# Where the shift row of the first attention values is kept, how it is added, and when the decay table is loaded, in a hybrid decoder block

## The chip, the cores and the metric

The kernel runs on one core of a Trainium2 chip, as one program with one launch. The metric is the device time of that core in microseconds; the runs of the kernel before gave 2195.38, 2193.04 and 2194.74 us, with a median of 2194.74 us. All data is float32; a matmul operand is split into a high and a low part, and every product is made as three matmuls.

## The reference

One decoder block on a sequence of 1024 tokens with a model width of 1024. A conditioning vector gives a shift and a scale for each channel. Two mixers read the same modulated input: chunkwise retention (4 heads) and dilated window attention (3 groups of 4 heads). Their outputs are gated, merged and projected, and an MLP with squared ReLU follows.

```python
def modulate(h, shift, scale):
    return h * (1 + scale[:, None, :]) + shift[:, None, :]

mod = jax.nn.silu(c) @ w_ada[l] + b_ada[l]
sh1, sc1, g1, sh2, sc2, g2 = jnp.split(mod, 6, axis=-1)
h = modulate(rms_norm(x, norm1_g[l]), sh1, sc1)
x = x + g1[:, None, :] * token_mixer(h, w_in[l], ...)
...
proj = h @ w_in
...
inner_decay = jnp.where(rel >= 0, jnp.exp(log_g[:, None, None] * jnp.maximum(rel, 0.0)), 0.0)
s = jnp.einsum('bhid,bhjd->bhij', qi, ki) * inner_decay[None]
```

Two places matter here. The attention values of the first group are `h @ w`, and since the shift is the same for every token, `shift @ w` is one row of 512 numbers that is added to all 1024 rows of the values. And retention multiplies its scores by a table of decays, one 128 x 128 block for each of the four heads.

## The kernel before

**Order.** The order of every engine is written out by hand; nothing is scheduled by a program. Each engine takes its instructions in that order and waits where an operand or a buffer is not ready. The DMAs of the weights, stores and copies are issued from SP's queue, one after another; DMAs that add to their destination (accumulating ones) are issued from GpSimd's queue. An issue that waits holds all issues behind it.

**Buffers.** Up to the retention, the tiles of 128 x 1024 come from `x4` (line 344): a ring of 26 buffers in SBUF that all kinds of tiles share. A new tile takes a buffer that was let go, and its first writer waits for the last readers of the tile that had it, DMAs among them. Which tile gets which buffer follows from the order in which tiles are made and let go. `decay` (128 x 512) is a tile of its own in another pool and keeps its place.

**First values** (`first_values` and `more_values`, to about 180 us). The values of attention group 0 are computed from the input before the shift is known to it, and stored to `va_d[0]` in DRAM, eight blocks of 128 rows x 512. Meanwhile `shift_rows` (line 996) sums on VectorE, over the eight blocks of input channels, weight row times shift into `decay`, which serves as scratch for that; so `decay` holds 128 partial rows. `more_values` then makes further values in eleven products of four parts. In the last product, after its first part, `shift_out` runs: one matmul with ones adds up the 128 partial rows and gives the shift row in all 128 partitions of a PSUM tile, two ScalarE copies put it twice, side by side, into the tile `shw` from the ring, and four accumulating DMAs of GpSimd add it to `va_d[0]`, 256 rows each.

**Pairs** (`queries_keys`, from about 180 us). 18 pairs of projections follow, numbered `q` from 0: queries and keys of the retention, queries of the attention, gates. A pair is made in a block scheme with seven products, in the order `11, s1, s3, s2, 12, 22, s4`, of 12 matmuls each, into the PSUM tiles `qap`. `Blocks.run` (line 302) does, for each product: its matmuls, then the preparation of weights some products ahead (sums of weight blocks on VectorE into `qas`, line 249; the high part by a ScalarE cast, line 254; the low part on VectorE, line 264, into `qaw`), then `post` (line 281). `post` copies and adds up PSUM tiles (`qat`, lines 286, 292 and 293) and hands finished blocks to `a_out` (line 1167), which writes the tiles `qa` (ScalarE, line 1182; VectorE, line 1184) and stores them. `a_load` (line 1142) loads the weight tiles `wa` two pairs ahead, and `copy_block` (line 531) sends copies and sums of other weights (`wrvs`, `wros`) to DRAM on the side, of which `quarter_sums` (line 539) are accumulating DMAs on GpSimd. In `after` (line 1226), at product 22 of pair 0, the decay table is loaded into `decay`, where the retention reads it (line 654).

Of the kernel before, what the change touches and what calls it, by code (L numbers as in the profile page):

```python
# [14 lines left out]
ALU = mybir.AluOpType  # L15
AX = mybir.AxisListType

P = 128
# [4 lines left out]
C = 128  # L23
NC = S // C
DV = 512
# [115 lines left out]
def block_kernel(ctx, tc, io, stop=None, dbg=None):  # L141
    nc = tc.nc
# [26 lines left out]
    def ps_s(name, shape=(P, 512)):  # L169
        return PS["p"].tile(list(shape), F32, tag="s", bufs=PS["n"], name=name)  # L170
# [168 lines left out]
    decay = right0.tile([P, H * C], F32, name="decay")  # L339
# [4 lines left out]
    def x4(name, dt=F32):  # L344
        return xpool.tile([P, 1024], dt, tag="x", bufs=26, name=name)
# [143 lines left out]
    def drain(gen):  # L489
        for _ in gen:  # L490
            pass
# [39 lines left out]
    def copy_block():  # L531

        if copies:
            d, src, n, j = copies.pop(0)
            nc.sync.dma_start(d[n][j], io[src][WB[n], j])
            if n == "s3":
                quarter_sums(d, io[src], j)
# [14 lines left out]
    def gn_signs():  # L552
        for i, v in enumerate((VC_GNG, VC_GNB)):
            nc.vector.tensor_copy(gnv[i][:, :16], vec[:, v:v + 16])
            nc.vector.tensor_scalar_mul(gnv[i][:, 16:], vec[:, v:v + 16], -1.0)
# [214 lines left out]
    va_d = [dram.tile([S, 512], F32, name=f"vad{g}") for g in range(3)]  # L770
# [233 lines left out]
    def shift_out():  # L1004

        ps = ps_s("shw")
        nc.tensor.matmul(ps, ones.to_broadcast([P, P]), decay, start=True, stop=True)
        t = x4("shw")
        for j in range(2):
            nc.scalar.copy(t[:, 512 * j:512 * j + 512], ps)  # L1010
        for i in range(4):
            dst = va_d[0][2 * C * i:2 * C * (i + 1)].rearrange("(a p) x -> p a x", p=P)
            nc.gpsimd.dma_start(dst, t.rearrange("p (a x) -> p a x", a=2), accum_op=ALU.add)

    def more_values(ahead):

# [24 lines left out]
        def pair_load(q):  # L1041
# [18 lines left out]
            (9, 0): [(sums_of_h, "t4", [0, 1]), (nc.sync.dma_start, cs, io["cossin"])],  # L1060
            (9, 1): [(sums_of_h, "t4", [2, 3])], (9, 2): [(late_low,), (pair_load, 0)],
            (10, 0): [(pair_load, 1), (shift_out,)],
        }
        for i in range(len(USEQ)):
# [77 lines left out]
    def a_load(q, part):  # L1142
        pair = PAIRS[q]
        src = io[{"g": "w_gate2", "a": "w_aq"}.get(pair[0]) or f"w_r{pair[1]}"]
        i = 2 * pair[1] + pair[2] if pair[0] == "a" else pair[-1]
        if q == 0 or q % 2 == 0 and part == 2:
            r = x4(f"wa{q}{part}")
        else:
            r = wraw.tile([P, 1024], F32, tag="raw", name=f"wa{q}{part}")
        nc.sync.dma_start(r, src[2 * i + part - 1])  # L1150
        BA.raw[q, part] = r
# [44 lines left out]
    def rotate(q):  # L1196

        _, t, h = PAIRS[q]
        u, v = BA.t[q]
        for hf in range(2):  # L1200
            hs = slice(512 * hf, 512 * hf + 512)
            x1, x2, cos, sin = OA[q][0][:, hs], OA[q][1][:, hs], cs[:, 0, hs], cs[:, 1, hs]
            for f, o, x, y in ((nc.vector.tensor_mul, u, x2, sin), (nc.vector.tensor_mul, v, x1, sin),
                               (nc.vector.tensor_mul, x1, x1, cos), (nc.vector.tensor_mul, x2, x2, cos),
                               (nc.vector.tensor_sub, x1, x1, u), (nc.vector.tensor_add, x2, x2, v)):
                f(o, x, y)
                yield
        for i in range(2):
            nc.sync.dma_start(qk_d[h][:, 2 * (t == "k") + i], OA[q][i])
# [4 lines left out]
    def queries_keys(ahead):  # L1214
        for _ in range(4):
            copy_block()
        sums = [(q, n) for q in range(NA) for n in ORDER][4:]

        def before(q, n):
            if n == ORDER[0] and q + 2 < NA:  # L1220
                for part in (1, 2):
                    a_load(q + 2, part)

        turns = []

        def after(q, n):

            if q == 0 and n == "22":
                gn_signs()
            if q == 0 and n == "22":  # L1230
                nc.sync.dma_start(decay, io["decay"])
            if n in ("s1", "s2", "12"):
                copy_block()
            if turns:
                next(turns[0], None) or None
            if n == ORDER[-1] and PAIRS[q][0] == "r":
                while turns:
                    drain(turns.pop())
                turns.append(rotate(q))
            if q == NA - 1 and n in ("s1", "s4"):  # L1240
                v_load(n == "s4")
            if q == NA - 1 and n == "12":
                v_base_load(0)
            if q == NA - 1 and n in ("12", "22"):
                v_w(0, int(n == "22"))
                v_low(0, int(n == "22"))

        BA.run([(q, n) for q in range(NA) for n in ORDER], sums, before, after, lambda q, n: n == "s2", lambda q: 1 if q == 0 else 2)
        while turns:
            drain(turns.pop())  # L1250
        values(ahead)
# [13 lines left out]
    def v_load(i):  # L1265

        hp, n = VSEQ[i]
        for j in range(2):
            lo = V["w", i, j] = v_place(i, "l", j)
            nc.sync.dma_start(fv(lo), wv_d[n][2 * hp + j])  # L1270

    def v_w(i, j):
        lo, hi, sign = V["w", i, j], v_place(i, "h", j), float(VPLAN[VSEQ[i][1]][1])
        nc.scalar.activation(hi, fv(lo), AF.Copy, scale=sign)
        V["w", i, j] = hi, lo
        V["low", i, j] = lo, hi, sign

    def v_low(i, j):
        lo, hi, sign = V.pop(("low", i, j))
        if sign > 0:  # L1280
            nc.vector.tensor_sub(lo, fv(lo), fv(hi))
        else:
            nc.vector.scalar_tensor_tensor(lo, fv(lo), -1.0, fv(hi), op0=ALU.mult, op1=ALU.subtract)
# [47 lines left out]
    def v_base_load(hp):  # L1331

        for j in range(2):
            V["m", hp, j] = t = x4(f"vm{hp}{j}")
            nc.sync.dma_start(t.rearrange("p (a b) -> p a b", a=2), m11_d[hp][:, 2 * j:2 * j + 2])

    def values(ahead):
        last = len(VSEQ) - 1
        for i, (hp, n) in enumerate(VSEQ):
            if i + 2 <= last:  # L1340
                v_load(i + 2)
            for p in range(4):
                v_mm(i, p)
                if V["post"]:
                    v_post(*V["post"].pop())
                V["post"].append((i, p))
                if i == 3 and p == 0:
                    v_base_load(1)
                if n == "s1" and p > 0:
                    v_base(hp, p - 1)  # L1350
                if n == "s2" and p == 0:
                    v_base(hp, 3)
                if p < 2 and i < last:
                    v_w(i + 1, p)
                    if p:
                        v_low(i + 1, 0)
                if p == 2 and i < last:
                    v_low(i + 1, 1)

                if i == last - 2 and p == 2:  # L1360
                    fetch(0)
                if i == last - 2 and p == 3:
                    first["release"]()
                if i == last - 1 and p in (1, 2):
                    jit_qk(p - 1)
                if i == last - 1 and p == 3:
                    ahead(2)
                if i == last and p == 0:
                    for m in range(4):
                        nc.gpsimd.dma_start(hh[2 * m][:, 512:], h12_d[m][:, 0])  # L1370
                        nc.gpsimd.dma_start(hl[2 * m][:, 512:], h12_d[m][:, 1])
        v_post(*V["post"].pop())
        open_ret()
        chunk_tiles()
        for g in (1, 2):
            fetch(g)
        R["sl"] = R["p"].tile([P, 2, DV], F32R, name="statel")
        R["sh"] = R["p"].tile([P, 2, DV], F32R, name="stateh")
        R["state"] = R["p"].tile([P, 2, DV], F32, name="state")
        banks(False)  # L1380
# [1423 lines left out]
```

## Time and profile before

| | value |
|---|---|
| runs, us | 2193.04, 2194.74, 2195.38 (median 2194.74) |
| the profiled execution's own time, us | 2194.82 |
| its span, first to last instruction, us | 2193.0 |
| mean granted TensorE clock | 0.996 |
| DMA packets, bytes | 160897, 416.78 MB |
| TensorE's first projections / retention / last stage | from 180 us / about 644 us / to the end of the span |

The profile is of one execution. In the views, a row of the timeline has the start, the duration, the engine and line, the operation with the tile it writes and the one it reads, and in brackets how long the engine had been idle before and what ended that. PE is TensorE's matmuls, PEld its weight loads, DVE is VectorE, ACT is ScalarE, POOL is GpSimd; SPq and POOLq are the queues that issue DMAs. Matmuls are pipelined: a row's duration overlaps the next, and the distance between two starts is what a matmul costs. The granted clock is a share of full speed.

### The profile page before, as it was taken

How to read it: one execution, taken by the hardware profiler on the slowest of the kernel's cores; microseconds unless marked ns; L12 is line 12 of the kernel's file. 1: busy time of each engine (PE TensorE's matmuls, PEld its weight loads, DVE VectorE, ACT ScalarE, POOL GpSimd, SP SyncE). 2: the span in 40 equal slices, each digit the busy share in tenths (PEclk: the TensorE clock that was granted, in tenths of full speed). 3: DMA queues.
4: the chain of work that ended last, by engine and by line, in shares of the span. 5: the costliest groups of instructions: out<-in, count | busy, mean ns of one | idle time of the engine just before them, and what ended most of it. 6: DMA issues, size and time to landing. Idle time of an engine off the chain costs nothing. (4 is left out here: it accounts for less than half of the span.)

```text
span 2193.0 us, 27323 instructions
## 1 busy us (share of the span) xinstructions
PE 2160.1 (98%) x10084; PEld 1794.8 (82%) x10084; DVE 1492.3 (68%) x2333; ACT 942.8 (43%) x1730; POOL 165.0 (8%) x196
## 2 busy tenths in 40 slices
PE   8998999999999999999999999999999999999998
PEld 6887788888878888888888888888778888888887
DVE  6984777775457878865565654777876665877855
ACT  5542322323434544544644634534454445533413
POOL 0001111100012221111100000001000000000003
PEclk9999999999999999999999999999999999999999
DMA  9869899834675555557763274654154435745322
GB/s 384 285 210 269 273 312 266 248 117 181 231 280 174 177 192 199 181 182 182 175 188 102 83 259 166 241 180 152 59 182 148 146 147 183 256 138 174 114 87 77
DMA packets 160897, 416.78 MB, mean 190 GB/s; under 512 B 27765, under 2 KB 55676, under 8 KB 157692
## 3 DMA queue, kind: packets, MB, share of 16 engines
q1 hardware_dynamic: 151416, 368.67, 47.5%
q0 software_dynamic: 9024, 46.14, 9.7%
q8 instruction: 79, 1.29, 0.2%
q14 instruction: 54, 0.44, 0.1%
q10 hardware_dynamic: 324, 0.23, 0.0%
HBM read 319.93 MB, written 156.13 MB: 217 GB/s over the span
## 5 line engine op out<-in xcount | busy, mean ns | idle before, releaser
L207 PE MATMUL qap<-hh,qaw 128*128 128x512 f32 x216 | 84.6, 392 | 2.4 <-DVE qat L293 2.4
L211 PE MATMUL qap<-hh,qaw 128*128 128x512 f32 x216 | 84.7, 392 | 0.0
L209 PE MATMUL qap<-hl,qaw 128*128 128x512 f32 x216 | 84.6, 392 | 0.0
L617 POOL TENSOR_TENSOR j<-qk,j 128x512 fp32r<-128x512 f32 x32 | 43.3, 1352 | 428.3 <-ACT j L616 410.3
L2124 POOL TENSOR_TENSOR accnf<-accnf,sqnf 128x256 f32<-128x256 f32 (+1 forms) x18 | 16.6, 921 | 609.6 <-ACT sqnf L2120 609.6
L2228 ACT ACTIVATE a<-a 128x512 f32<-128x512 f32 x48 | 30.3, 631 | 73.7 <-DVE a L2227 73.7
L1544 ACT ACTIVATE P<-P,ng 128x128 f32<-128x128 f32 (+1 forms) x96 | 41.9, 438 | 36.9 <-DVE ng L1541 33.3
L2436 ACT CAST w2h<-w2s 128x512 fp32r<-128x512 f32 x36 | 22.4, 622 | 79.4 <-DVE w2s L2474 79.4
L264 DVE TENSOR_TENSOR fw<-w1r,fw 128x512 fp32r<-128x512 f32 x48 | 32.9, 688 | 33.5 <-ACT fw L254 33.5
L207 PEld LDWEIGHTS qap<-hh,qaw 128*128 128x128 f32 x216 | 40.8, 189 | 11.3 <-DVE qat L293 2.8
L207 PE MATMUL fp<-h2h,fw 128*128 128x512 f32 x128 | 50.0, 391 | 0.0
L1959 DVE TENSOR_TENSOR rwl<-rwl,rwh 128x1024 fp32r<-128x1024 f32 x25 | 30.2, 1220 | 29.0 <-ACT rwh L1989 29.0
L211 PE MATMUL fp<-h2h,fw 128*128 128x512 f32 x128 | 49.8, 389 | 0.0
L209 PE MATMUL fp<-h2l,fw 128*128 128x512 f32 x128 | 49.8, 389 | 0.0
L207 PE MATMUL roa<-rh,rwl 128*128 128x512 f32 x128 | 49.8, 389 | 0.0
L209 PE MATMUL roa<-rl,rwh 128*128 128x512 f32 x128 | 49.8, 389 | 0.0
L211 PE MATMUL roa<-rh,rwh 128*128 128x512 f32 x128 | 49.8, 389 | 0.0
L652 ACT COPY sm<-sT 128x128 f32<-128x128 f32 x32 | 8.5, 265 | 93.9 <-PE sT L640 93.9
L211 PEld LDWEIGHTS qap<-hh,qaw 128*128 128x128 f32 x216 | 40.8, 189 | 8.6
L209 PEld LDWEIGHTS qap<-hl,qaw 128*128 128x128 f32 x216 | 40.8, 189 | 8.4
L2124 POOL TENSOR_TENSOR accn<-accn,sqn 128x512 f32<-128x512 f32 x12 | 15.5, 1293 | 385.9 <-ACT sqn L2120 385.9
L1949 ACT ACTIVATE rh<-rl 128x512 fp32r<-128x512 f32 x56 | 31.7, 625 | 23.4 <-PE roc L209 8.4
(3097 smaller groups left out, 7258.8 us busy)
## 6 DMA issues: line engine op xcount, KB each, us to landing
v<-vd SPq DMA_DIRECT2D x32, 512.0 KB, 4.4
raw<-in_w_ada_dram SPq DMA_DIRECT2D x32, 512.0 KB, 5.1
w1r<-in_w_ff_dram SPq DMA_DIRECT2D x32, 512.0 KB, 4.5
yt<-y POOLq DMA_DIRECT2D x24, 512.0 KB, 7.3
xsd<-as SPq DMA_DIRECT2D x24, 512.0 KB, 2.8
w2r<-in_w_ff2s_dram SPq DMA_DIRECT2D x24, 512.0 KB, 6.7
em<-in_w_ada_dram SPq DMA_DIRECT2D x16, 512.0 KB, 10.2
wrvs<-in_w_rv_dram POOLq DMA_DIRECT2D x16, 512.0 KB, 9.3
```

Of the source, the lines that this page charges most:

```text
L207: nc.tensor.matmul(o, wl, xh, start=first, stop=False, skip_group_check=skip)
L209: nc.tensor.matmul(o, wh, xl, start=False, stop=False, skip_group_check=skip)
L211: nc.tensor.matmul(o, wh, xh, start=False, stop=last, skip_group_check=skip)
L264: nc.vector.tensor_sub(t[:, 512:], src, fv(t[:, :512]))
L617: nc.gpsimd.tensor_sub(t[:, 1], src, fv(t[:, 0]))
L652: nc.scalar.copy(sm, ps[:, :C])
L1544: nc.scalar.activation(v, v, AF.Exp, bias=ng[:, blk:blk + 1], accum_out=st[:, g, blk, 2 + a:3 + a])
L1949: nc.scalar.activation(hi, fv(lo), AF.Copy, scale=sign)
L1959: nc.vector.tensor_sub(lo, fv(lo), fv(hi))
L2124: (nc.vector if f == 7 else nc.gpsimd).tensor_add(G["acc", key], G["acc", key], sq)
L2228: nc.scalar.activation(o, o, AF.Relu)
L2436: nc.scalar.copy(hi, src)
```

## The change

The sum of the shift row goes back into `decay` itself, one copy of 512 numbers in each partition in place of two in a tile of the ring. The DMAs read it there with a stride of zero over the blocks of rows: three DMAs of 3, 3 and 2 blocks in place of four of 2. As `decay` is now read by these DMAs, the decay table, which goes into the same tile, is loaded three pairs later: at product 22 of pair 3.

```diff
         ps = ps_s("shw")
         nc.tensor.matmul(ps, ones.to_broadcast([P, P]), decay, start=True, stop=True)
-        t = x4("shw")
-        for j in range(2):
-            nc.scalar.copy(t[:, 512 * j:512 * j + 512], ps)
-        for i in range(4):
-            dst = va_d[0][2 * C * i:2 * C * (i + 1)].rearrange("(a p) x -> p a x", p=P)
-            nc.gpsimd.dma_start(dst, t.rearrange("p (a x) -> p a x", a=2), accum_op=ALU.add)
+        nc.scalar.copy(decay, ps)
+        for i, n in ((0, 3), (3, 3), (6, 2)):
+            dst = va_d[0][C * i:C * (i + n)].rearrange("(a p) x -> p a x", p=P)
+            nc.gpsimd.dma_start(dst, decay[:, None, :].to_broadcast([P, n, DV]), accum_op=ALU.add)
...
-            if q == 0 and n == "22":
+            if q == 3 and n == "22":
                 nc.sync.dma_start(decay, io["decay"])
```

No tile of the ring is made for the shift row, so the tiles made after it take other buffers than before; the order of the instructions on the engines is the same but for the lines of the diff.

## The prediction

> **What bounds the kernel now.** I began with the page: how long the run is, and which engine fills it.
>
> ```profile
> span 2193.0 us, 27323 instructions
> PE 2160.1 (98%) x10084; PEld 1794.8 (82%) x10084; DVE 1492.3 (68%) x2333; ACT 942.8 (43%) x1730; POOL 165.0 (8%) x196
> ```
>
> TensorE is busy for 98% of the span, so an edit is worth only what it does to TensorE's idle or slow time. The changed lines lie near 170 to 190 us (sums of the shift row, table load) and near 270 us (the table's new place). So next I read the busy times by stretch around them; the columns are PE, PEld, DVE, ACT and POOL busy time, then the granted clock, DMA share and GB/s.
>
> ```profile
> 200.00:210.00 10.00, 4.91 (x22) 3.75 (x20) 0.20 (x1) 1.10 (x2) 2.91 (x3) 0.86 0.79 132
> 210.00:220.00 10.00, 9.45 (x34) 7.70 (x35) 8.58 (x18) 3.58 (x7) 1.30 (x2) 0.80 0.75 199
> 220.00:230.00 10.00, 7.60 (x26) 5.74 (x25) 9.56 (x16) 4.21 (x8) 0.52 (x1) 0.83 0.75 244
> 230.00:240.00 10.00, 10.00 (x45) 8.28 (x45) 7.88 (x14) 3.39 (x6) 2.37 (x3) 1.00 0.86 207
> 240.00:300.00 60.00, 60.00 (x266) 49.68 (x265) 43.11 (x69) 18.32 (x31) 7.82 (x12) 1.00 0.96 323
> ```
>
> From 240 us on TensorE is full at clock 1.00; from 200 to 230 us it is neither. TensorE's list of waits names two causes (total, times, longest).
>
> ```profile
> PE qap L207 <- DVE qaw1s L264: 5.6, 1, 5.6
> PE qap L207 <- DVE qat L293: 2.4, 1, 2.4
> ```
>
> To price that hole I use the kernel's own period. A pair of projections is seven products of 12 matmuls, always in one order, so the first matmul of product s1 marks each pair. The timeline gives these marks for pairs 0, 1, 2 and 3, and between them the two halts.
>
> ```profile
> 182.99 0.39 PE L207 MATMUL qap<-xat,qaw0s 128*128 128x512 f32 x1
> ...
> 202.03 0.39 PE L207 MATMUL qap<-xat,qaw1s 128*128 128x512 f32 x1
> ...
> 204.53 0.39 PE L211 MATMUL qap<-xat,qaw1s 128*128 128x512 f32 x1
> 210.55 0.80 PE L207 MATMUL qap<-xat,qaw1s 128*128 128x512 f32 x1 [5.64 <-DVE qaw1s L264]
> ...
> 220.25 0.39 PE L211 MATMUL qap<-hh,qaw 128*128 128x512 f32 x1
> 223.04 0.50 PE L207 MATMUL qap<-hh,qaw 128*128 128x512 f32 x1 [2.40 <-DVE qat L293]
> ...
> 233.00 0.39 PE L207 MATMUL qap<-xat,qaw2s 128*128 128x512 f32 x1
> ...
> 252.04 0.39 PE L207 MATMUL qap<-xat,qaw3s 128*128 128x512 f32 x1
> ```
>
> Pair 0 to 1 takes 202.03 - 182.99 = 19.04 us and 2 to 3 takes 252.04 - 233.00 = 19.04 us; pair 1 to 2 takes 30.97 us. The hole costs 30.97 - 19.04 = **11.93 us**. At 19.04/84 = 0.227 us a matmul, the halts are 210.55 - 204.53 - 0.23 = 5.79 us and 223.04 - 220.25 - 0.23 = 2.56 us; the other 3.58 us is the stretch of low clock after each, 1.8 us apiece.
>
> What holds the first halt is seen on ScalarE and VectorE.
>
> ```profile
> 195.33 0.62 ACT L254 CAST qaw1s<-qas 128x512 fp32r<-128x512 f32 x1 [8.47 <-DVE qas L249]
> 208.67 0.60 ACT L1182 ACTIVATE qa<-qap 128x512 f32<-128x512 f32 x1 [12.72 <-DMA vad<-shw]
> 209.16 0.61 ACT L254 CAST qaw1s<-qas 128x512 fp32r<-128x512 f32 x1
> ...
> 196.59 0.68 DVE L249 TENSOR_TENSOR qas<-wa,wa 128x512 f32<-128x512 f32 x1
> 209.81 0.69 DVE L264 TENSOR_TENSOR qaw1s<-qas,qaw1s 128x512 fp32r<-128x512 f32 x1 [12.53 <-ACT qaw1s L254]
> ```
>
> ScalarE's copy of a finished product into `qa` sits for 12.72 us, because its output took the buffer of `shw`, which the four summing DMAs still read. Behind it in ScalarE's order stands the cast of pair 1's s3 weights, behind that VectorE's low part, behind that TensorE. VectorE then works off a backlog (9.56 of 10 us busy), and the second halt is its late `qat`:
>
> ```profile
> 221.58 0.68 DVE L292 TENSOR_TENSOR qat<-qat,qap 128x512 f32<-128x512 f32 x1
> 222.29 0.69 DVE L293 TENSOR_TENSOR qat<-qap,qat 128x512 f32<-128x512 f32 x1
> ```
>
> Product s2 ended about 217.9 us, so these came 3.7 us late. Both halts have one root.
>
> **The change part by part.**
>
> *The tile.* `shw` and one of its two copies go (0.59 us each; ScalarE had been idle 8.5 us there, so this saves the path nothing). The sum is copied into `decay`, which is not in the ring of 26 buffers. As built, the copy into `qa` gets another buffer and waits for no summing DMA, but for the store of an attention value from the product before the pairs (SP's order, then the time to landing of those stores: least, median, most):
>
> ```profile
> 174.39 7.03 SPq L994 DMA_DIRECT2D vad<-ur  x4
> ```
> ```profile
> DMA to landing us min/median/max: 3.7/4.6/5.5
> ```
>
> That store is the first of the four and lands by 174.4 + 5.5 = 179.9 us; ScalarE comes to the copy at 195.33 + 0.62 = 195.95 us, and its input is ready at about 194.1 (pair 0's product 12 ends four products of 2.72 us after 182.99). So it runs at 195.95. The cast of s3 follows VectorE's sum (196.59 + 0.68 = 197.3), VectorE's low part ends near 198.6, and TensorE wants it at 204.76: 6 us to spare. The first halt goes, with it the backlog and the second halt. Gain: 11.93 us.
>
> *The DMAs.* Four of 512 KB become two of 768 and one of 512 KB: the same 1024 rows of 2 KB. GpSimd issued them one by one, the next only when the one before had landed:
>
> ```profile
> 173.68 1.43 POOL L1013 DMA_DIRECT2D vad<-shw  x1 [127.31 <-DMA vad<-ur]
> 181.02 1.24 POOL L1013 DMA_DIRECT2D vad<-shw  x1 [5.91 <-issue]
> 193.22 1.21 POOL L1013 DMA_DIRECT2D vad<-shw  x1 [10.97 <-issue]
> 202.52 1.22 POOL L1013 DMA_DIRECT2D vad<-shw  x1 [8.09 <-issue]
> 203.26 2.17 POOL L543 DMA_DIRECT2D wrvs<-in_w_rv_dram  x2
> ```
>
> All four took 208.67 - 173.68 = 35.0 us. If each DMA costs the same, three take 26 us; if bytes count, 35 us. They start 0.6 us earlier, so they land at 199 to 208 us; I take 208, the rows being of equal bytes. No row shows an accumulating DMA that repeats its source. The nearest repeats a row from DRAM (KB each, us to landing), beside a plain store:
>
> ```profile
> biasd<-browd SPq DMA_DIRECT2D x12, 192.0 KB, 6.6
> vad<-ur SPq DMA_DIRECT2D x16, 256.0 KB, 4.0
> ```
>
> Per KB it is (6.6/192)/(4.0/256) = 2.2 times a plain store. That bounds the sums from above: 2.2 x 35 = 77 us, landing at 250 us. Behind them on GpSimd's queue stand the quarter sums of the weights (L543 to L549). GpSimd is through with them by 450 us:
>
> ```profile
> 450.00:500.00 50.00, 50.00 (x222) 41.40 (x221) 36.75 (x59) 13.53 (x24) 0.00 (x0) 1.00 0.27 93
> ```
>
> They are read in the last pair, 17, from 252.04 - 2.7 + 14 x 19.04 = 516 us, so a shift of either sign is covered.
>
> *The table.* Its load leaves SP's queue at 189.87 and goes between the two stores of pair 3, past the loads and copies of pairs 3 to 5 (SP's order, then the line that reads the table):
>
> ```profile
> 189.87 0.33 SPq L1231 DMA_DIRECT2D decay<-in_decay_dram  x1
> ...
> 269.57 3.56 SPq L1194 DMA_DIRECT2D gated<-qa  x2
> 273.23 1.05 SPq L1150 DMA_DIRECT2D wa<-in_w_rk_dram  x2
> ```
> ```profile
> L654 DVE TENSOR_TENSOR sm<-sm,decay x32: 291/292/295, 647.7 to 944.0; 128x128 f32<-128x128 f32 x32
> ```
>
> With TensorE 11.9 us ahead it stands at about 257.7 us. It now waits for the three sums, with pair 3's second store and pair 6's weights queued behind it. By 208 us, or the bound of 250, the wait is met: cost nothing but 0.33 us of issue. Its first reader comes at 647.7 - 11.9 = 635.8, hundreds of us later.
>
> *What the earlier pace takes.* DMA share from 200 to 240 us is 7.9 + 7.5 + 7.5 + 8.6 = 31.5 us of 40. In 28.1 us this would be 112%: 3.4 us of transfers are pushed into 240 to 300 us, where the share is 0.96. VectorE had no slack there once:
>
> ```profile
> 249.54 0.69 DVE L249 TENSOR_TENSOR qas<-wa 128x512 f32<-128x512 f32 x1 [0.40 <-DMA wa<-in_w_rq_dram]
> ```
>
> Those are pair 4's weights, wanted by TensorE at 252.04 + 19.04 = 271.1 us, so 3.4 us of lateness is hidden unless it holds VectorE's evictions. Cost taken: 0; bound: one halt like the second, 2.56 + 1.8 = 4.4 us.
>
> *After 300 us* TensorE is full, so the 11.9 us carry to the end. **Sum:** the profiled execution took 2194.82 us (span 2193.0 and 1.8 around it; the three runs' median is 2194.74, so it is a typical one). 2194.8 - 11.9 = **2182.9 us**.
>
> The low clock after the second halt is 0.83 in 220:230 although the halt was 2.56 us. The Trainium skill, "TensorE: Matmul & The Clock Gate", section "Part 1: The HAM clock gate", has the clock fall after an idle window of about 3.4 us. By it the halt would have cost 2.56 us and not 4.4, and a like one in rival 1 as much. The trace goes against it here, and the row decides.
>
> **The rivals.**
>
> 1. *A halt comes back, made by DMA.* The 3.4 us of displaced transfers hold VectorE at a weight tile while an eviction is due. For it: share 0.96 and the 0.40 us wait. Against: no halt in 240:300 at that share. Price up to 4.4 us: 2187.3.
>
> 2. *The copy waits all the same*, on its new store or on something not seen. Against: that store landed 16 us before. Time: no change, 2194.8.
>
> 3. *Slower: the sums with repeated source crawl and SP stands.* If repeating three copies confined a DMA to three of the 16 engines, the sums would take 35.0 x 16/3 = 187 us and land near 360. SP would stand at the table from 257.7 to 360. Pair 6's weights, wanted by TensorE at 252.04 - 2.7 + 57.1 - 11.9 = 294.5, would come at 360 + 11 + 3 (landing as in the row below, and the first casts): TensorE waits 79 us, 2262. It costs something once SP is freed later than 280 us (3.1 times the old duration) and more than the gain from 292 us (3.4 times). Against: the 2.2 bound, and that the pattern's outer dimension is the 128 partitions in both forms.
>
> ```profile
> DMA to landing us min/median/max: 9.5/10.9/12.2
> ```
>
> The Trainium skill, "DMA: Bandwidth & Descriptors", section "Rules for kernel authors", states this rule: a leading zero-stride broadcast of c copies confines a DMA to at most c engines. By it an access pattern with the copies outermost gives 2262; as built they stand in the middle, and by the same rule all 16 engines stay in use, which leaves 2182.9. No row shows either.
>
> **How the numbers follow.** Forecast 76%, rival 1 14%, rival 2 4%, rival 3 4%; 2% for what I don't see. The forecast's own spread is about 2.4 us to either side, as the runs shown (2193.04 to 2195.38) differ by 2.3. The forecast alone is short of 8 in 10, so the range runs from 2182.9 - 2.4 = 2180.5 past rival 1's 2187.3 to 2188.5; beyond it lie rivals 2 and 3. 0.2% is 4.4 us, about what measurement can tell from no change; faster means below 2190.4: forecast and rival 1, 0.90. Same: rival 2 and 1%, 0.05. Slower: rival 3 and 1%, 0.05.
>
> **What would show each step.** Right: the s1 marks of pairs 0 to 3 all 19.04 us apart; no `qa` wait on a DMA near 196 us; TensorE's list without `qaw1s` and `qat`; clock 1.00 in every 10 us from 180 to 300; the three sums landed by 210 us; SP issuing the table within a microsecond of pair 3's first store. Wrong: a pair of more than 20 us before 450 us, VectorE idle on `wa` with TensorE behind it, or an SP queue that stands at the table. If the marks hold and the end is still above 2188, the gain was given back later, and the busy time after 450 us would show where.

## The result and the profile after

The changed kernel takes 2182.7 us (median of 6 runs, 2181.87 to 2184.25); the kernel before, run on the same chip, takes 2194.11 us (6 runs, 2192.77 to 2195.38). The ratio is 0.9949 with a 95% interval of 0.9936 to 0.9962: faster by 11.4 us, or 0.5%. The profiled execution took 2182.64 us.

The page of the changed kernel, its length and the busy times of the engines:

```profile
span 2180.9 us, 27323 instructions
PE 2156.0 (99%) x10084; PEld 1791.6 (82%) x10084; DVE 1491.7 (68%) x2333; ACT 942.8 (43%) x1729; POOL 164.0 (8%) x195
```

The span is 2193.0 - 2180.9 = 12.1 us shorter, and ScalarE and GpSimd have one instruction fewer each. Where the time came from is seen in the busy times by stretch around the pairs 0 to 3 (the same columns as before):

```profile
200.00:210.00 10.00, 10.00 (x46) 8.29 (x45) 8.09 (x14) 4.62 (x8) 2.94 (x3) 1.00 0.68 145
210.00:220.00 10.00, 10.00 (x45) 8.26 (x45) 9.46 (x16) 3.30 (x6) 0.53 (x1) 1.00 1.00 333
220.00:230.00 10.00, 10.00 (x46) 8.27 (x45) 7.58 (x13) 3.40 (x6) 1.29 (x2) 1.00 1.02 312
230.00:240.00 10.00, 10.00 (x46) 8.28 (x45) 8.48 (x14) 2.25 (x4) 2.39 (x3) 1.00 0.87 269
```

TensorE is busy for all of each 10 us at clock 1.00, where it had been busy for 4.91, 9.45 and 7.60 us at 0.86, 0.80 and 0.83. The marks (first matmul of product s1) of pairs 0 to 3 in the timeline:

```profile
182.84 0.39 PE L207 MATMUL qap<-xat,qaw0s 128*128 128x512 f32 x1
...
201.88 0.39 PE L207 MATMUL qap<-xat,qaw1s 128*128 128x512 f32 x1
...
220.92 0.39 PE L207 MATMUL qap<-xat,qaw2s 128*128 128x512 f32 x1
...
239.96 0.39 PE L207 MATMUL qap<-xat,qaw3s 128*128 128x512 f32 x1
```

All are 19.04 us apart: the 30.97 us from pair 1 to pair 2 are now 19.04. ScalarE's order in the same stretch, and VectorE's low part behind it:

```profile
195.17 0.62 ACT L254 CAST qaw1s<-qas 128x512 fp32r<-128x512 f32 x1 [8.53 <-DVE qas L249]
195.70 0.59 ACT L1180 ACTIVATE qa<-qap 128x512 f32<-128x512 f32 x1
197.15 0.62 ACT L254 CAST qaw1s<-qas 128x512 fp32r<-128x512 f32 x1 [0.86 <-DVE qas L249]
...
197.81 0.69 DVE L264 TENSOR_TENSOR qaw1s<-qas,qaw1s 128x512 fp32r<-128x512 f32 x1 [0.69 <-ACT qaw1s L254]
```

The copy into `qa` (line 1180 in the changed kernel, which is two lines shorter) follows the cast without a wait. Before, it stood for 12.72 us. The low part of s3 is done at 198.50 us where it had been done at 210.50. In TensorE's list of waits `qaw1s` and `qat` are gone; its top rows are waits from elsewhere in the kernel:

```profile
PE pb L441 <- DMA onehot<-in_onehot_dram: 5.2, 2, 3.8
PE fp L209 <- DVE xt L2264: 2.0, 2, 1.1
```

The three sums on GpSimd, and the table on SP's queue between the two stores of pair 3:

```profile
173.04 1.51 POOL L1011 DMA_DIRECT2D vad<-decay  x1 [126.25 <-DMA vad<-ur]
183.91 1.31 POOL L1011 DMA_DIRECT2D vad<-decay  x1 [9.36 <-DMA vad<-ur]
202.13 1.22 POOL L1011 DMA_DIRECT2D vad<-decay  x1 [16.91 <-issue]
...
257.48 0.33 SPq L1192 DMA_DIRECT2D gated<-qa  x1
258.00 0.35 SPq L1229 DMA_DIRECT2D decay<-in_decay_dram  x1
```

The third sum was issued at 202.1 us, as late as the fourth had been (202.52): three DMAs of more rows take about as long as four. The sums became no faster that can be seen; ScalarE no longer stands behind them.

### The profile page after: what moved, and what is told of

Same layout as the page of the kernel before. It is cut to its first block, busy times and chain, and to the rows that moved or that the text cites. A ratio compares the mean times of both kernels' runs of the same rounds, so it can differ in the third digit from the quotient of the medians.

```text
span 2180.9 us, 27323 instructions
## 1 busy us (share of the span) xinstructions
PE 2156.0 (99%) x10084; PEld 1791.6 (82%) x10084; DVE 1491.7 (68%) x2333; ACT 942.8 (43%) x1729; POOL 164.0 (8%) x195
## 6 DMA issues: line engine op xcount, KB each, us to landing
em<-in_w_ada_dram SPq DMA_DIRECT2D x16, 512.0 KB, 10.2
```

## The experiments

The theory to be tested: the whole gain is that ScalarE's copy into `qa` no longer takes over a buffer which the sums read; number of DMAs, zero stride and the table's place give nothing by themselves. The rivals put some or all of the gain into those parts. In every run below, "hole" is the distance between the marks of pairs 1 and 2 less 19.04 us.

**The sums kept, the buffer taken away.** The kernel before, with `shw` in a tile that no pair inherits:

```diff
-        t = x4("shw")
+        t = cb
```

> The kernel before with the tile `shw` taken outside the ring: the two copies go into `cb`, a tile of the same size in another pool, and the four DMAs read it there. (What `cb` held is lost, so the later modulations read the shift row in place of the conditioning vector; no instruction is added or removed.) Four DMAs, two copies, table at pair 0 as before; no tile of the ring inherits a buffer that the sums read. My theory: no tile waits for the sums, marks 19.04 us apart, 2183 us (2181 to 2185). Rival A (the fewer DMAs, the zero stride or the later table are needed): 2194. Rival B (they make a part): 2186 to 2191.

Measured: 2182.86 us (4 runs, 2182.34 to 2184.51), ratio to before 0.9948 (0.9931 to 0.9964): all of the gain, with four DMAs, two copies, no zero stride and the table at pair 0. GpSimd and ScalarE in its timeline:

```profile
204.77 1.22 POOL L1013 DMA_DIRECT2D vad<-cb  x1 [9.29 <-issue]
...
196.74 0.62 ACT L254 CAST qaw1s<-qas 128x512 fp32r<-128x512 f32 x1 [8.52 <-DVE qas L249]
197.27 0.59 ACT L1182 ACTIVATE qa<-qap 128x512 f32<-128x512 f32 x1
```

The fourth sum was issued 7.5 us after the copy had run; no engine of the pairs waited for it. Rivals A and B fall.

**The wait put back into the changed kernel.**

```diff
         if y is None:
+            if q == 0:
+                nc.scalar.copy(decay[:, :1], cb[:, :1])
             nc.scalar.activation(o, view(x), f)
```

> The changed kernel with the wait put back by hand: ahead of ScalarE's copy into pair 0's `qa`, ScalarE writes one column of `decay`, which the three sums still read, so it waits until they have landed (the column is written over by the table load later). My theory: the sums land at 207 to 211 us, the copy and the cast of s3 behind it come 12 to 15 us late, both halts come back, 2194 to 2198 us. Rival (the wait was only a symptom, and the fewer DMAs or the moved table made the gain): 2183 to 2187.

Measured: 2193.07 us (10 runs, 2191.09 to 2194.40), ratio 0.9991 (0.9982 to 1.0000). The profiled execution is the shortest of them. Its timeline:

```profile
206.90 0.19 ACT L1181 COPY decay<-cb 128x1 f32<-128x1 f32 x1 [10.45 <-DMA vad<-decay]
207.01 0.60 ACT L1182 ACTIVATE qa<-qap 128x512 f32<-128x512 f32 x1
...
208.89 0.80 PE L207 MATMUL qap<-xat,qaw1s 128*128 128x512 f32 x1 [3.47 <-DVE qaw1s L264]
...
221.37 0.50 PE L207 MATMUL qap<-hh,qaw 128*128 128x512 f32 x1 [1.26 <-DVE qat L293]
```

Both halts are back. They are shorter: the sums landed 1.8 us earlier than before (206.9 against 208.67), and the clock stayed at 1.00 behind the second halt; the hole is 229.69 - 202.53 - 19.04 = 8.12 us. With three DMAs, the zero stride and the late table all in place, one wait for one column takes nearly all of the gain away. The median is 0.9 us below my range. In the profiled execution the sums landed at the lower end of what I had expected, and no low clock followed the second halt.

**The table alone.** The kernel before with the load moved to pair 3:

```diff
-            if q == 0 and n == "22":
+            if q == 3 and n == "22":
                 nc.sync.dma_start(decay, io["decay"])
```

> The kernel before with only the table load moved from pair 0 to pair 3. My theory: the copy into `qa` still waits for the four sums, 2194 us (2192 to 2196). Rival (256 KB less in the crowded stretch lets the sums land earlier): the sums land some us before 208 us and the time is 2189 to 2192.

Measured: 2194.2 us (10 runs), ratio 0.9996 (0.9987 to 1.0006): no change. ScalarE's copy still waits, as the timeline shows:

```profile
209.59 0.60 ACT L1182 ACTIVATE qa<-qap 128x512 f32<-128x512 f32 x1 [13.09 <-DMA vad<-shw]
```

**The tile alone.** The changed kernel with the load back at pair 0 (the edit above, the other way round).

> The changed kernel with the table load back at pair 0. It now has to wait for the three sums on SP's queue, with pair 2's and 3's weights behind it. My theory: SP stands from about 190 to the landing at 207 to 211 us, pair 3's weights are issued some 5 us later than in the changed kernel and still in time, 2183 us (2181 to 2185). Rival (the move of the table is needed): SP's standing makes weights late, VectorE waits on `wa`, and a halt of 2 to 6 us comes back: 2186 to 2192.

Measured: 2183.5 us (4 runs), ratio 0.9948 (0.9933 to 0.9963). SP's queue in its timeline:

```profile
186.30 1.90 SPq L535 DMA_DIRECT2D wrvs<-in_w_rv_dram  x3
209.13 0.33 SPq L1229 DMA_DIRECT2D decay<-in_decay_dram  x1
209.56 0.91 SPq L1148 DMA_DIRECT2D wa<-in_w_gate_dram  x2
```

SP does stand at the table until the sums have landed (209.13 us, marks 1.0 us later than in the changed kernel), and pair 3's weights are issued 6 us later than there. The timeline of the changed kernel has them at:

```profile
203.25 1.54 SPq L1148 DMA_DIRECT2D wa<-in_w_gate_dram  x2
```

They are still in time: the marks of pairs 1 and 2 are at 202.89 and 221.93 us, 19.04 us apart. So the table's later place is worth nothing here. It removes a wait that had cover.

**Another buffer by way of a dummy tile.** The kernel before with

```diff
         if q not in OA:
+            if q == 0:
+                d = x4("dum")
+                nc.gpsimd.memset(d[:, :1], 0.0)
             OA[q] = [x4(f"qa{q}{i}") for i in range(2)]
```

> The kernel before with one thing added: when pair 0 makes its two `qa` tiles, a dummy tile of the ring is made ahead of them and one column of it is zeroed on GpSimd. The four DMAs from `shw`, the two copies and the table load stay as they were; only the buffers move up by one, so that ScalarE's copy into `qa` inherits a buffer whose reader is a store of attention values and not the four sums. My theory (the whole gain is that this copy no longer waits for the sums): the copy runs near 196 us, both halts go, the marks of pairs 0 to 3 are 19.04 us apart, 2183 us (2181 to 2185). Rival A (the gain needs the fewer DMAs, the zero stride or the later table): 2194, with the hole of 11.9 us still there. Rival B (part of the gain is the DMAs): 2186 to 2191.

Measured: 2224.8 us (4 runs), ratio 1.0135 (1.012 to 1.015): slower, and a miss for me. Two rows of its timeline, of VectorE and ScalarE, tell why:

```profile
209.90 0.69 DVE L249 TENSOR_TENSOR qas<-wa 128x512 f32<-128x512 f32 x1 [15.53 <-DMA vad<-shw]
...
255.11 0.62 ACT L254 CAST qaw2s<-qas 128x512 fp32r<-128x512 f32 x1 [25.60 <-POOL dum L1173]
```

The edit shifted every tile behind it in the ring. The buffer of `shw` went to `qas`, so now VectorE stood 15.53 us behind the sums; and the dummy's one column was zeroed only when GpSimd's queue came to it at 254.71 us, with ScalarE waiting 25.60 us for that. The edit is not the clean test that I meant it to be. It does show that the wait went with the buffer.

**How much lateness costs.** With the wait put back, two sums in place of three, and four:

```diff
-        for i, n in ((0, 3), (3, 3), (6, 2)):
+        for i, n in ((0, 3), (3, 3)):
```

> The changed kernel with the wait put back, but only two of the three sums (rows 768 to 1023 of the first values lack the shift row). In the run with the wait and all three sums the third was issued at 200.8 us, when the second had landed; so the copy into `qa` goes on near 201.5 us, 5 to 6 us late. My theory (lateness costs only beyond the 6 us of slack): no halt on `qaw1s`, at most a halt of up to 2 us on `qat` from VectorE's smaller backlog, 2183 to 2186 us. Rival (the cost grows with the waiting from the first microsecond, so 5.5 of 10.5 us cost half of the hole): a hole near 5 us, 2188.

Measured: 2186.16 us (6 runs, 2181.86 to 2189.81), ratio 0.9963 (0.9950 to 0.9976). The profiled execution took 2188.5 us. Its timeline:

```profile
202.57 0.60 ACT L1182 ACTIVATE qa<-qap 128x512 f32<-128x512 f32 x1
...
216.94 0.57 PE L207 MATMUL qap<-hh,qaw 128*128 128x512 f32 x1 [3.75 <-DVE qat L293]
```

There is no halt on `qaw1s`, as expected, but one of 3.75 us on `qat`, twice what I had allowed; the hole is 226.84 - 202.12 - 19.04 = 5.68 us. My theory missed: the slack of the weights holds, and another, smaller one behind it does not. The rival's figures, a hole near 5 us and 2188 us, fit this execution; its reason, a cost from the first microsecond on, falls with the run with two copies below, where a copy 2.0 us late costs nothing. Three of the six runs took 2187.89 to 2189.81 us and three 2181.86 to 2184.43, so the median lies between two groups and only the slower one has a trace.

```diff
-        for i, n in ((0, 3), (3, 3), (6, 2)):
+        for i, n in ((0, 3), (3, 3), (6, 2), (0, 3)):
```

> The changed kernel with the wait put back and a fourth sum of 768 KB (rows 0 to 383 get the shift row twice). The four land near 214 to 220 us in place of 206.9. My theory: beyond the slack every microsecond of landing is a microsecond of the end; from the hole of 8.1 us at 206.9 it grows to 15 to 21 us: 2198 to 2204 us. Rival (a halt of any length costs about the same, most of the hole being the clock and the backlog): 2193 to 2196.

Measured: 2198.63 us (10 runs, 2197.12 to 2202.71), ratio 1.0021 (1.0012 to 1.0030). Its timeline:

```profile
215.52 0.60 ACT L1182 ACTIVATE qa<-qap 128x512 f32<-128x512 f32 x1
...
217.40 0.79 PE L207 MATMUL qap<-xat,qaw1s 128*128 128x512 f32 x1 [11.83 <-DVE qaw1s L264]
...
229.88 0.50 PE L207 MATMUL qap<-hh,qaw 128*128 128x512 f32 x1 [1.94 <-DVE qat L293]
```

From the run with three sums to this one the copy comes 215.52 - 207.01 = 8.5 us later and the hole grows from 8.12 to 238.19 - 202.69 - 19.04 = 16.46, by 8.3 us. Between these two runs it is one for one.

**The same lateness without a DMA.** The changed kernel with `n` copies on ScalarE ahead of the one into `qa`:

```diff
         if y is None:
+            for _ in range(n if q == 0 else 0):
+                nc.scalar.copy(cb, cb)
             nc.scalar.activation(o, view(x), f)
```

Nine copies:

> The changed kernel with nine copies of `cb` onto itself (128 x 1024, about 1.0 us each) on ScalarE ahead of pair 0's copy into `qa`: the same lateness made without any DMA. My theory: the cast of s3 comes about 9.3 us late, of which 6 to 7 are covered, so TensorE halts on `qaw1s` for 2 to 3 us. Before, a halt of 2.4 us was followed by a low clock, halts of 1.3 and 1.4 us in the runs with other waits were not: if the clock falls, 1.8 us more, 2186.5 to 2188; if it needs a window of 3.4 us, 2184.5 to 2186. Rival (only a wait on a DMA halts TensorE, the slack is larger): 2183.

Measured: 2190.58 us in one run, against a median of 2194.79 for the kernel before. ScalarE and TensorE in its timeline, then its busy times by stretch:

```profile
195.61 9.71 ACT L1181 COPY cb<-cb 128x1024 f32<-128x1024 f32 x9
205.22 0.59 ACT L1182 ACTIVATE qa<-qap 128x512 f32<-128x512 f32 x1
...
207.09 0.50 PE L207 MATMUL qap<-xat,qaw1s 128*128 128x512 f32 x1 [2.43 <-DVE qaw1s L264]
...
219.47 0.50 PE L207 MATMUL qap<-hh,qaw 128*128 128x512 f32 x1 [3.71 <-DVE qat L293]
```
```profile
200.00:210.00 10.00, 7.57 (x34) 5.74 (x32) 2.96 (x9) 7.61 (x10) 0.84 (x2) 1.00 1.00 208
210.00:220.00 10.00, 6.29 (x27) 4.89 (x27) 9.16 (x15) 3.08 (x6) 1.29 (x2) 1.00 0.82 262
220.00:230.00 10.00, 10.00 (x38) 8.10 (x37) 9.09 (x16) 3.90 (x7) 2.39 (x3) 0.83 0.65 170
```

The first halt is 2.43 us, inside the 2 to 3 that I expected, and the clock stayed at 1.00 behind it. The second, 3.71 us on `qat` with a low clock behind it, I had not expected: the time is 2.6 us above the upper of my two ranges. No DMA is in this chain, so lateness by itself makes the halts.

Two and five copies, to find the slack of `qat`:

> The changed kernel with two copies of `cb` onto itself ahead of pair 0's copy into `qa`: the cast of s3 comes about 1.3 us late. From the runs with more lateness I work out that the weights have 6 us of slack, but VectorE's `qat` after product s2 only about 2 us. My theory: no halt, 2183 us. Rival (no slack at all on VectorE, which is busy for 8 to 9.5 of 10 us here): a halt of about 1 us on `qat`, 2184 to 2185.

> The changed kernel with five such copies: the cast of s3 comes about 4.5 us late, within the slack of the weights (6 us) and beyond that of `qat` (2 us). My revised theory: no halt on `qaw1s`, one halt of 2.2 to 2.8 us on `qat` near 213 us; 2185.3 without and 2187 with a low clock behind it. Rival (the 6 us of the prediction hold for all that follows): no halt, 2183.

Measured: 2182.19 and 2184.93 us, one run each, beside a median of 2195.62 for the kernel before. With two there is no halt. With five, in the timeline:

```profile
202.14 0.61 ACT L254 CAST qaw1s<-qas 128x512 fp32r<-128x512 f32 x1
...
215.91 0.50 PE L207 MATMUL qap<-hh,qaw 128*128 128x512 f32 x1 [2.31 <-DVE qat L293]
```
```profile
210.00:220.00 10.00, 7.69 (x34) 6.02 (x34) 9.70 (x16) 3.43 (x7) 0.53 (x1) 1.00 1.04 360
220.00:230.00 10.00, 10.00 (x46) 8.28 (x45) 8.43 (x15) 3.35 (x6) 1.30 (x2) 1.00 0.77 202
```

One halt, on `qat` alone, no fall of the clock, a hole of 224.21 - 202.56 - 19.04 = 2.61 us: the revised theory. In the changed kernel itself the rows for this slack are:

```profile
210.24 0.69 DVE L292 TENSOR_TENSOR qat<-qat,qap 128x512 f32<-128x512 f32 x1 [0.59 <-PE qap L211]
210.96 0.69 DVE L293 TENSOR_TENSOR qat<-qap,qat 128x512 f32<-128x512 f32 x1
```

VectorE was idle for 0.59 us ahead of `qat` and done at 211.65. From the halt with five copies (TensorE stopped there 213.21 + 0.23 - 202.56 = 10.88 us after its mark) TensorE wants it at 201.88 + 10.88 = 212.76. So 1.1 us and 0.59 of idle time are what VectorE has to spare, 1.7 us of lateness of the cast. The run with five copies gives the same: counted from the mark, its cast of s3 came (202.14 - 202.56) - (197.15 - 201.88) = 4.31 us later than in the changed kernel, and the hole is 2.61.

**The sums doubled, with nobody waiting.** The changed kernel with

```diff
-        for i, n in ((0, 3), (3, 3), (6, 2)):
+        for i, n in ((0, 3), (3, 3), (6, 2)) * 2:
```

> The changed kernel with the three sums issued twice (the shift row is added twice to the first values): 4 MB of accumulating transfers in place of 2 MB, and no engine but SP's and GpSimd's queues waits for them. My theory (what the sums move and when they land costs nothing so long as no tile of the pairs waits for them): they land near 230 to 245 us, the table still leaves SP's queue near 258 us, marks 19.04 us apart, 2183 us (2181 to 2185). Rival (transfers pushed into 240 to 300 us make weights late, as in rival 1 of the prediction): one halt or more, 2186 to 2190.

Measured: 2183.39 us (4 runs, 2182.41 to 2183.66), ratio 0.9946 (0.9930 to 0.9963), as the changed kernel. GpSimd, SP's queue and TensorE in its timeline:

```profile
228.66 1.21 POOL L1011 DMA_DIRECT2D vad<-decay  x1 [8.28 <-issue]
...
258.96 0.33 SPq L1229 DMA_DIRECT2D decay<-in_decay_dram  x1
...
221.82 0.39 PE L207 MATMUL qap<-xat,qaw2s 128*128 128x512 f32 x1
...
240.86 0.39 PE L207 MATMUL qap<-xat,qaw3s 128*128 128x512 f32 x1
```

The last sum is issued 26.5 us later than in the changed kernel, twice the bytes go through, and the marks stay 19.04 us apart. This rival falls too. The sums had still landed before SP came to the table, so SP did not stand here.

The profiled executions on one line each (without the dummy tile, where other engines wait), with the time that ScalarE's copy into `qa` started after the cast ahead of it had let go (its start + 0.52), and the hole:

| run | copy late by, us | halts on `qaw1s`, `qat`, us | hole, us |
|---|---|---|---|
| changed kernel; buffer taken away; table at pair 0; sums doubled | 0 | none | 0 |
| two copies | 2.0 | none | 0 |
| five copies | 5.3 | 0, 2.31 | 2.6 |
| wait, two sums | 6.6 | 0, 3.75 | 5.7 |
| nine copies | 9.6 | 2.43, 3.71 | 8.5 |
| wait, three sums | 10.7 | 3.47, 1.26 | 8.1 |
| kernel before | 12.8 | 5.64, 2.40 | 11.9 |
| table alone | 13.2 | 6.00, 2.38 | 12.3 |
| wait, four sums | 19.0 | 11.83, 1.94 | 16.5 |

Where there is a hole, it is shorter than the lateness of the copy: by 2.5 to 2.7 us with five copies and with the wait and three or four sums, by 0.9 to 1.1 us in the other four rows. What sets the two groups apart is the clock after the halt on `qat`. In the first group it stayed at 1.00. In the second it fell to half for about 3.4 us, which costs 1.7. A low clock after the first halt does not lengthen the hole: in the run with the wait and three sums TensorE restarted at 208.89 us and ran at half clock until 214.8, and that hole is still 2.6 us shorter than the lateness. TensorE would have met VectorE's backlog next all the same.

## Why the prediction was right

**The hole and its one root.** The 11.93 us were priced from the marks, and 12.1 us of span came off. That both halts have one root is shown from both sides: the buffer taken away from `qa` removes both with the four DMAs, the two copies and the early table still in place, and the wait put back brings both back.

**The low clock.** The prediction put 1.8 us of low clock beside each halt. As an account of where TensorE's time went, it holds. As a price, the table shows that only the fall after the halt on `qat` made the hole longer; the one after the first halt was hidden by VectorE's backlog. The forecast did not depend on it, since the hole was priced whole.

**The copy.** Forecast at 195.95 us, it ran at 195.70; the low part was forecast for 198.6 and ended at 198.50, with pair 1's mark at 201.88.

**"6 us to spare".** This step was right for what it named, the weights of s3: 198.50 against 201.88 + 12 x 0.227 = 204.60. But it named the wrong place as the tightest. `qat` has only 1.7 us of the cast's lateness to spare, as the run with five copies shows. The forecast did not suffer, since the copy has no lateness left at all: here the number did not test the step. Had the cast stayed 4 us late, the forecast would by my estimate have been about 2 us too low.

**The DMAs.** The choice of equal bytes over equal DMAs came out: 35.0 us for four, and for three 206.90 - 173.70 = 33.2 us in the run with the wait and at most 209.13 - 174.05 = 35.1 in the run with the table at pair 0, not 26. In the changed kernel itself no row shows the landing. The bound of 2.2 for the repeated source was far too wide. That repeating costs nothing by itself is not shown: it came together with the fewer DMAs, and what one cost the other may have saved.

**The table.** Forecast at 257.7 us in SP's queue, it left at 258.00, its wait long met. As costed, it is worth nothing. The kernel with the table back at pair 0 is as fast.

**The displaced transfers.** The DMA share of the stretch from 200 to 240 us rose to 6.8 + 10.0 + 10.2 + 8.7 = 35.7 us of 40. Counted by the pairs, as the prediction did, the 28.1 us from 200 on had a share of 0.87, so 24.4 us of the 31.5; some 7 us of transfers moved later and not 3.4, and the next 60 us had a share of 0.99. The term was too small, but the cost taken, 0, is what happened, and the doubled sums show that there was room for 2 MB more.

**The sum.** 2182.9 us against 2182.64 in the profiled execution and a median of 2182.7.

**The rivals.** The first (a halt by DMA) and the third (SP stands until the weights are late) did not come; the run with the doubled sums went toward the first and found nothing, and the run with the table at pair 0 let SP stand for 21 us without harm. How long SP may stand before it costs something was not reached in any run. Rival 2 (the copy waits all the same) did not come either; the run with the wait put back shows what it would have looked like. A pattern with the copies outermost, to which rival 3's three engines would have applied, was not tried.

## What to carry to other kernels

A tile from a shared ring hands its slowest reader to whichever tile takes its buffer next; where a long DMA reads a short-lived tile, ask who inherits the buffer, and keep such tiles outside the ring that a critical engine draws from. The gain lies in the wait and not in the transfer: with the wait in place, fewer DMAs or other loads moved out of their way left 0.9991 and 0.9996 of the time before, and doubling them cost nothing once nobody stood behind them. When slack is counted, follow the late engine's whole order to the next things it owes, not only the first; and a dummy tile is a poor way to move one ring buffer, since it moved the waits of the tiles behind it too (2224.8 us).

## What the runs showed of the hardware that was not expected

A halt's length alone did not decide whether the clock fell. The second halt of the kernel before (2.40 us in the list of waits) was followed by a granted clock of 0.83 in 220 to 230 us; the first halt of the run with nine copies (2.43 us) and the one of the run with five (2.31 us) were followed by 1.00. The Trainium skill, "TensorE: Matmul & The Clock Gate", section "Part 1: The HAM clock gate", describes a free-running window of about 3.4 us that is not aligned to the program, and a fall after an idle window of that length. The traces show such a window. In the kernel before, the clock was at half from 207.2 to 214.0 us and from 224.3 to 227.7; these stretches and the time between them last 6.8, 3.4 and 10.2 us, all multiples of 3.4. They do not bear out that it has to be idle throughout. In the 3.41 us ahead of each of its two falls TensorE was busy for 1.12 and 1.22 us, and ahead of those in the run with the table alone for 0.71 and 1.27. In the run with nine copies, counted back in steps of 3.41 us from its fall at 220.12, the two windows that share the first halt had 1.61 and 2.79 us of busy time, and the clock stayed. So where a halt lies in these windows decides with its length. By these few rows, the border is between 1.27 and 1.61 us of busy time in 3.41; whether anything else counts stays open.

The runs in which an engine waits for the sums also spread more: 2181.86 to 2189.81 us with two sums and the wait, against 2181.87 to 2184.25 for the changed kernel. I take this for the landing time of the sums, which moves from one execution to the next (the last one was issued between 197.38 and 203.34 us in the six profiled executions that issue the same three sums); it was not measured by itself.
